# A hybrid decoder step on one core: the second chunk's rows loaded ahead of the value weights, the extra tokens' gates from float32 weights, maxima and first gates in another PSUM group

## The chip, the core and the metric

The kernel runs on one core of one Trainium2 chip. The core has five engines that each take their instructions in order: TensorE (PE, matrix products), VectorE (DVE, elementwise work and reductions), ScalarE (ACT, activations and scaled copies), GpSimd (POOL) and SyncE (SP, which here issues all the transfers). Products land in PSUM, a small memory of eight banks; everything else lies in SBUF. Sixteen DMA engines move data between device memory and SBUF.

The metric is the device time of one execution in microseconds (us). "Before" is the median of three executions. A profile is one further execution, taken by the hardware profiler, and its span is the time from its first to its last instruction.

## What is computed

One layer of a decoder for 2048 prompt tokens in 16 chunks of 128, with 48 extra tokens: 32 sample tokens (8 sequences of 4) and 16 meta tokens. All have 1024 features. Each token is layer-normed and goes through one combined projection; half of the width is an mLSTM evaluated chunk by chunk, the other half is sliding-window attention; both are gated, projected out and merged with the residual. Cut to what matters here:

```python
hp = layer_norm(concat([meta, x_prompt]), ln0_g, ln0_b)
hs = layer_norm(x_sample, ln0_g, ln0_b)
mq, mk, mv, mo, mz, mi, mf, aq, ak, av, az = split_proj(h @ w_in + b_in)

def mlstm_chunk(state, q, k, v, log_i, log_f):      # log_i = mi, log_f = log_sigmoid(mf)
    c, n, m = state
    b = cumsum(log_f)
    dmat = where(causal, b[:, None] - b[None, :] + log_i[None, :], -inf)
    inter = b + m
    m_t = maximum(inter, max(dmat))                 # running-max stabiliser
    w, s_inter = exp(dmat - m_t), exp(inter - m_t)
    ...
```

The meta tokens form a leading chunk, so the state with which the first prompt chunk starts depends on their gates `mi`, `mf` (four heads each, eight columns of the projection). The sample tokens start from given states `st_c`, `st_n`, `st_m`.

## The kernel before

**Precision by splitting.** Most products are made in float16 with a high and a low part: a weight matrix is loaded in float32 into four staging tiles, its largest magnitude is found, and it is scaled by a power of two and split into two float16 halves. `prep_steps` (L242) does this: a reduction for each quarter on ACT (L257) or DVE (L259), `all_max` (L128) over the partitions, `pow2` (L118), then for each quarter a scaled copy on ACT (L271) and a subtraction on DVE (L274). `all_max` multiplies the identity by each partition's maximum (L134, into `dg`, one buffer), sends it through a float32 matmul with ones (L135) into a PSUM tile, and reduces that on DVE (L136).

**PSUM.** Eight banks are shared by four groups: `pj` (2 buffers, projections), `pt` (3, transposes, scores, maxima, gates), `px` (1, extra tokens) and `po` (2), which is first used at L639.

**Phase A** runs over the chunks: layer norm and transposition (`norm_x`, L392, two chunks ahead of their use), projections q, k, v, o and gates, and the mLSTM recurrence (`m_rows` to `m_kv`). Between its steps the work of the extra tokens and the preparation of the second phase's weights are interleaved (`jobs`, L1060). **Phase B** runs over the chunks again for the attention and the output projection.

**The start of phase A** is the part that the change touches. The first chunk's rows `x0` are normed (L443), transposed in float32 (L448, copies L449) and multiplied with the unsplit float32 weights (`proj32`, L413), since split weights don't exist yet. `a_proj(0, i, st)` (L417) does this for q, k, v and o with the staging tiles `stq`, `stk`, `stv`, `sto`. The first two lie in different pools: q's and v's staging share the four buffers of tag "stg", so v's loads (L551, L552) wait until q's tiles have been read. k's and o's have buffers of tag "w" (name `stage`).

The extra tokens `xe` are normed (L556), split (`split_e`, L382) and transposed by a DMA into `ET`; `proj_e` (L301) multiplies them with split weights, high and low part stacked in one product. Before, their gates are made in the same way: `proj_e(ge, ET, wg, 8, bg, t1, ps=pt)` (L578), after `wg` has been prepared (L569). Then come the log-sigmoid (`log_sigmoid_rows`, L465: 15 small DVE operations and an exponential), two transposes (L581, L582), the scans for meta and sample tokens (L588 to L614) with the load `mS` of the sample states (L599) and four stores of the new ones (L616), three transposes (L619) and `tok` (L621).

x0 itself is also split and transposed for later (L561 to L563, stored by L622) and its normed rows are stored (L564). `xs`, the buffer of incoming rows, has two buffers: x0 and xe take both, so x1 (L565, L566) waits for one of them.

**What sets the order.** The code is traced once and a planner then places every instruction: the earlier in the code the higher its rank, but work that is ready goes to an engine that is free. Loads written with `first` (L108) form a chain: each is issued on SP after the one before it. Transfers written with `dma` (L98) are free until `Order.anchor` is set (L567), and after that are issued behind the anchor.

Of the kernel before, what the change touches and what calls it, by code (L numbers as in the profile page):

```python
# [16 lines left out]
P = 128  # L17
D = 1024
# [23 lines left out]
def tile_hymba_step(  # L42
# [22 lines left out]
    def pt(shape):  # L65
        return psum("pt", shape, 3)
# [4 lines left out]
    def po(shape):  # L71
        return psum("po", shape, 2)
# [8 lines left out]
    def work(tag, shape, dt=F32, bufs=None):  # L81
        return mn.tile(shape, dt, tag=tag, name=tag, bufs=bufs or KB4.get(tag, 1))
# [10 lines left out]

    class Order:
        last = None
        anchor = None

    def dma(out, in_, start=None):  # L98
# [9 lines left out]
    def first(out, in_, start=None):  # L108
        start = start or S.dma_start
        if Order.last is None:  # L110
            Order.last = start(out=out, in_=in_).ins
            return
        with tc.issue_after(Order.last):
            c = start(out=out, in_=in_).ins
        Order.last = c
# [12 lines left out]
    def all_max(a, m):  # L128

        n = m.shape[1]  # L130
        ps = pt([P, n, P])
        for i in range(n):
            d = small("dg", P, bufs=1)
            V.tensor_scalar(d, ident, m[:, i:i + 1], None, op0=ALU.mult)  # L134
            T.matmul(ps[:, i], ones, d, start=True, stop=True)  # L135
        V.tensor_reduce(a, ps, axis=AX.X, op=ALU.max)  # L136
        return a
# [9 lines left out]
    def bias_tile(off, n, dma=dma):  # L147
        b = work("bias", [P, n], bufs=4)
        dma(b, b_in[0:1, off:off + n].partition_broadcast(P))
        return b  # L150
# [23 lines left out]
    def stage(n, tag="stg"):  # L174

        if tag == "w":
            t = wp.tile([P, KT, n], F32, tag="w", name="stage")
            return [t[:, 2 * i:2 * i + 2, :] for i in range(4)]
        return [work("stg", [P, 2, n]) for _ in range(4)]

    def load(st, src, parts=range(4), dma=first):
        for i in parts:
            dma(st[i], src[:, 2 * i:2 * i + 2, :])
# [7 lines left out]
    load(stq, w_a[0])  # L191
    xe = work("xs", [P, D])[:NE]
    first(xe, x_e)
    stk = stage(512, "w")
    load(stk, w_a[1])
    bA = [bias_tile(0, 512, first), bias_tile(512, 512, first)]
    tg = cst.tile([P, KT, 8], F32, name="tg")
    first(tg, w_g)
    bg = cst.tile([P, 8], F32, name="bg")
    first(bg, b_in[0:1, 2560:2568].partition_broadcast(P))  # L200


    caus = cs[:, C_CAUS:C_CAUS + P]
# [252 lines left out]
    def scale_qk(i):  # L456

        m = small("bd", 1)
        V.tensor_scalar(m, wA[i].mx, xnorm, 32.0, op0=ALU.mult, op1=ALU.mult)
        V.tensor_tensor(m, m, bqk[:, i:i + 1], op=ALU.add)  # L460
        a, b = pow2(m, f"pq{i}", 2.0 ** -40)
        s_qk.append(a)
        i_qk.append(b)
# [36 lines left out]
    def a_gate(n):  # L500
        c = ca[n]
        gts = small("gts", 8)
        if n == 0:
            ps = pt([P, 8])
            proj32(ps, lambda k: tg[:, k])
            V.tensor_tensor(gts, ps, bg, op=ALU.add)
            log_sigmoid_rows(gts, P, 0)
            return
        ps = pt([P, 16])
        for k in range(KT):  # L510
            T.matmul(ps, c.xT[:, k, :], wg.t[:, k].rearrange("p c n -> p (c n)"), start=(k == 0), stop=False,
                     skip_group_check=True)
        for k in range(KT):
            T.matmul(ps[:, 0:8], c.xT[:, KT + k, :], wg.t[:, k, 0], start=False, stop=(k == KT - 1),
                     skip_group_check=True)
        V.scalar_tensor_tensor(gts, ps[:, 8:16], wg.ev, bg, op0=ALU.mult, op1=ALU.add)
        V.scalar_tensor_tensor(gts, ps[:, 0:8], wg.ev, gts, op0=ALU.mult, op1=ALU.add)
        log_sigmoid_rows(gts, P, n % 2)
# [29 lines left out]
    bA[3] = bias_tile(1536, 512, first)  # L548
    wA[0] = prep("q", stq, 512, sums=(0, 1, 2))
    scale_qk(0)  # L550
    stv = stage(512)  # L551
    load(stv, w_a[2])  # L552
    bA[2] = bias_tile(1024, 512, first)
# [2 lines left out]
    ln0_(xe, NE, hl.rearrange("p c d -> p (c d)").bitcast(BF16)[:NE])  # L556
    split_e(EE[:, 0], xe, NE, s_x)
    dmat(ET, EE[:, 0])
    first(cs[:, P:], consts[:, P:])
    xT0 = work("xT", [P, 2 * KT, P], F16)  # L560
    A.activation(hl[:, 0], x0, AF.Copy, scale=s_x)  # L561
    V.scalar_tensor_tensor(hl[:, 1], x0, s_x, hl[:, 0], op0=ALU.mult, op1=ALU.subtract)
    dmat(xT0, hl.rearrange("p c d -> p (c d)"))  # L563
    dma(h_d[0], x0)  # L564
    x1 = work("xs", [P, D])  # L565
    first(x1, x_p[P:2 * P, :])  # L566
    Order.anchor = Order.last  # L567
    a_proj(0, 0, stq)
    wg = prep("g", [tg[:, 2 * i:2 * i + 2, :] for i in range(4)], 8)  # L569
    a_gate(0)  # L570
    last = proj_e(qe, ET, wA[0], 512, bA[0], t1)
    dma(e_d[:, 0], qe)
    wA[1] = prep("k", stk, 512, sums=(0,2))
    scale_qk(1)
    sc_qk = col()
    V.tensor_scalar(sc_qk, i_qk[1], QSC, None, op0=ALU.mult)
    a_proj(0, 1, stk)
    last = proj_e(ge, ET, wg, 8, bg, t1, ps=pt)  # L578
    log_sigmoid_rows(ge, NE, 1)
    pr = pt([P, 2, P])  # L580
    T.transpose(pr[:, 0, :NE], Gf[1][:NE, :], ident[:NE, :NE])  # L581
# [37 lines left out]
        T.transpose(ptr[:NE, i, :], rows[:, i, :], ident)  # L619
    tok = ea.take(12)[:NE].rearrange("p (c h) -> p c h", h=H)  # L620
    V.tensor_copy(tok, ptr[:NE, :, 0:P:32])  # L621
    dma(xT_d[0], xT0)  # L622
    dma(he_d, xe)
    a_proj(0, 2, stv)
# [450 lines left out]
        return int(done[0]) > a  # L1075

    extra = jobs()
    carry.mark = None

    def a_steps(n):  # L1080
# [427 lines left out]
```

## Time and profile before

| | us |
|---|---|
| median of three executions | 1077.33 |
| lowest, highest | 1075.49, 1078.78 |
| the profiled execution, its own time | 1080.81 |
| its span, first to last instruction | 1079.0 |
| mean granted TensorE clock, share of full speed | 0.984 |

The profile gives for each instruction its engine, the line of the kernel, the tile that it writes and those that it reads, its start, its duration, and what ended the idle time of its engine before it. `xs<-in_dram` is a transfer of device memory into the tile `xs`; "SPq" is the queue in which SP issues transfers. PE is TensorE's stream of matmuls and PEld its weight loads. A float32 matmul shows as two instructions. Matmuls are pipelined, so the time from one start to the next, not the duration, is what one costs in a row of them. The granted clock is the share of full speed at which TensorE was allowed to run.

### The profile page before, as it was taken

The page shows a single profiled execution, that of the slowest core. Times are in us where ns is not written, and L with a number is a line of the kernel's source. Part 1 is how long each engine was busy: PE and PEld are TensorE (multiplying, and loading weights), DVE is VectorE, ACT ScalarE, POOL GpSimd, SP SyncE. Part 2 cuts the span into 40 slices and gives each one's busy share as a digit, 9 for nine tenths or more (in the row PEclk, how much of TensorE's full clock was granted, in tenths as well). Part 3 has the DMA queues.
Part 4 walks back from the last instruction along what each step waited for, and adds up shares of the span by engine and source line. Part 5 has one row for each costly group of instructions (what it writes and reads, how often), then busy time and mean ns, then how long its engine had stood idle before and what let it go on. Part 6 is the DMA issues. An engine that isn't in the chain of part 4 may idle for free.

```text
span 1079.0 us, 17626 instructions
## 1 busy us (share of the span) xinstructions
PE 1035.4 (96%) x6391; PEld 573.5 (53%) x6391; DVE 730.5 (68%) x2057; ACT 442.6 (41%) x1112; POOL 254.0 (24%) x270
## 2 busy tenths in 40 slices
PE   6979998999999998998999999999999999999996
PEld 3435565655555554555564554555555555555553
DVE  5769666776867796877546686566666566666674
ACT  5646332244444445462234343433343433343430
POOL 2112231321120001113011141333322333322322
PEclk9998999999999998999999999999999999999998
DMA  9756447345785686655686455546445645545452
GB/s 323 202 141 164 110 120 173 97 126 145 232 235 143 190 239 168 208 132 145 232 265 112 79 131 127 137 119 126 102 123 125 132 115 131 110 110 131 113 122 63
DMA packets 245809, 161.83 MB, mean 150 GB/s; under 512 B 207945, under 2 KB 220953, under 8 KB 244409
## 3 DMA queue, kind: packets, MB, share of 16 engines
q1 hardware_dynamic: 245722, 160.70, 57.3%
q8 instruction: 50, 0.82, 0.3%
q14 instruction: 37, 0.30, 0.1%
HBM read 68.22 MB, written 43.58 MB: 104 GB/s over the span
## 4 chain that ended last, share of the span: by engine, by line
PE 65%; DMA 12%; DVE 11%; issue 5%; ACT 4%; POOL 1%; SPq 1%; DVEq 0%; ACTq 0%; POOLq 0%
PE pj L1341 15%; PE pj L299 13%; PE pj L296 12%; PE pj L297 12%; PE pt L1261 3%; DMA xT<-hl 2%; PE po L1314 2%; DMA ea<-in_dram 2%; DMA stg<-hl 1%; DMA kT<-kh 1%; DVE xs L380 1%; DMA wd_o<-w_o 1%; PE px L725 1%; ACT hl L323 1%; DMA da<-e_d 1%
## 5 line engine op out<-in xcount | busy, mean ns | idle before, releaser
L296 PEld LDWEIGHTS <-xT 128*128 128x128 f16 x992 | 98.0, 99 | 103.9 <-issue 7.5
L299 PEld LDWEIGHTS <-xT 128*128 128x128 f16 x992 | 97.0, 98 | 98.3 <-issue 2.9
L297 PEld LDWEIGHTS <-xT 128*128 128x128 f16 x992 | 98.0, 99 | 94.8 <-issue 4.3
L1341 PEld LDWEIGHTS <-EE 128*128 128x128 f16 x720 | 70.8, 98 | 80.3 <-issue 2.2
L1341 PE MATMUL pj<-w_o,EE 128*128 128x512 f16 x360 | 83.7, 384 | 0.0
L1341 PE MATMUL pj<-wr_o,EE 128*128 128x512 f16 x360 | 82.3, 379 | 0.0
L1268 ACT ACTIVATE SI<-SI,nb 128x272 f32<-128x272 f32 (+1 forms) x64 | 32.4, 507 | 66.1 <-DVE nb L1265 66.0
L325 POOL TENSOR_TENSOR lns<-lns,mhalf 128x1 f32<-128x1 f32 (+1 forms) x16 | 20.1, 1256 | 136.9 <-ACT lns L324 123.9
L296 PE MATMUL pj<-w_q,xT 128*128 128x512 f16 x120 | 46.4, 387 | 4.8 <-DMA xT<-hl 4.8
L1274 POOL TENSOR_TENSOR mhl<-SI,mhl 128x32 f16<-128x32 f32 x32 | 13.7, 430 | 157.3 <-ACT mhl L1273 157.3
L783 POOL TENSOR_TENSOR qs<-qT 128x512 f32<-128x512 f16 x16 | 23.2, 1453 | 113.5 <-DMA qT<-qh 50.1
L1268 ACT ACTIVATE g<-g,nb 128x272 f32<-128x272 f32 (+1 forms) x64 | 32.1, 503 | 42.7 <-DVE nb L1265 42.7
L296 PE MATMUL pj<-wr_z,xT 128*128 128x512 f16 x128 | 49.3, 385 | 0.0
L297 PE MATMUL pj<-wr_z,xT 128*128 128x512 f16 x128 | 49.2, 384 | 0.0
L296 PE MATMUL pj<-wr_az,xT 128*128 128x512 f16 x128 | 48.5, 379 | 0.0
L296 PE MATMUL pj<-wr_aq,xT 128*128 128x512 f16 x128 | 48.5, 379 | 0.0
L297 PE MATMUL pj<-wr_aq,xT 128*128 128x512 f16 x128 | 48.5, 379 | 0.0
L297 PE MATMUL pj<-wr_az,xT 128*128 128x512 f16 x128 | 48.5, 379 | 0.0
L296 PE MATMUL pj<-w_o,xT 128*128 128x512 f16 x120 | 47.3, 394 | 0.0
L297 PE MATMUL pj<-w_o,xT 128*128 128x512 f16 x120 | 47.1, 393 | 0.0
L1171 POOL TENSOR_TENSOR xs<-xs,gb 128x1024 f32<-128x1024 f32 (+1 forms) x16 | 42.8, 2675 | 15.4 <-DMA stg<-hl 9.3
L296 PE MATMUL pj<-w_v,xT 128*128 128x512 f16 x120 | 46.4, 386 | 0.0
(459 smaller groups left out, 2506.1 us busy)
## 6 DMA issues: line engine op xcount, KB each, us to landing
stg<-in_dram SPq DMA_DIRECT2D x28, 512.0 KB
xs<-in_dram SPq DMA_DIRECT2D x16, 512.0 KB
h_d<-xs SPq DMA_DIRECT2D x16, 512.0 KB
xT_d<-xT SPq DMA_DIRECT2D x16, 512.0 KB
xs<-h_d SPq DMA_DIRECT2D x16, 512.0 KB
xT<-xT_d SPq DMA_DIRECT2D x16, 512.0 KB
out_dram<-xs SPq DMA_DIRECT2D x15, 512.0 KB
hn_d<-g SPq DMA_DIRECT2D x16, 258.0 KB
```

Source lines behind the costliest of these rows:

```text
L296: T.matmul(ps, xT[:, k, :], w.t[:, k, 0, :n], start=(k == 0), stop=False)
L297: T.matmul(ps, xT[:, k, :], w.t[:, k, 1, :n], start=False, stop=False)
L299: T.matmul(ps, xT[:, KT + k, :], w.t[:, k, 0, :n], start=False, stop=(k == KT - 1))
L323: A.activation(junk[:, D:2 * D], x, AF.Square, bias=nmu, accum_out=ss)
L325: G.tensor_tensor(rs, ve, mhalf[:rows, 0:1], op=ALU.pow)
L783: G.tensor_tensor(c.qs, c.qT[:, 0], c.qT[:, 1], op=ALU.add)
L1171: G.tensor_tensor(z, z, lg[:rows], op=ALU.mult)
L1261: T.matmul(ps[:, lo:], c.qT[:, h], kTs[:, 2 * (h // 4) + x, lo:], start=(x == 0), stop=(x == 1))
L1268: A.activation(p[:, i, lo:], p[:, i, lo:], AF.Exp, bias=nb[:, h:h + 1], accum_out=sums[:, h:h + 1])
L1274: G.tensor_tensor(m[:, 1], p[:, :, 2 * P:], m[:, 0], op=ALU.subtract)
L1314: T.matmul(pso[:, h], l, r, start=False, stop=(i == len(last) - 1), skip_group_check=True)
L1341: T.matmul(ps, c.yT[:, a, :], w[:, k, t, :], start=(first and j == 0), stop=(last and j == len(mm) - 1))
```

## The change

- `all_max` takes its PSUM tile from `po` until a flag `Order.running` is set, which happens where phase A's loop begins, and from `pt` after that. The first chunk's gates (`a_gate(0)`) take theirs from `po`.
- The loads of the gate weights `tg`, their bias `bg` and the constants move ahead of the loads of k's weights and of the biases of q and k.
- x1 is allocated and loaded ahead of v's staging loads, and so ahead of the bias behind them; before, it came after these and after the constants. The anchor is set at the same place relative to x0's store; it is now v's bias, no longer x1.
- The extra tokens' gates no longer use `proj_e` with split weights. `xe` is transposed by eight TensorE transposes into one PSUM tile, copied by ACT to `xef`, and multiplied with the float32 weights `tg` in eight matmuls; DVE adds the bias.
- This part, with the log-sigmoid, the scans, `mS`, the stores and `tok`, now stands ahead of x0's split and transposition, of the first chunk's q and k projections and of the preparation of the gate and k weights; before, it stood behind them.

```diff
--- before.py
+++ after.py
@@ -93,6 +93,7 @@
 
     class Order:
         last = None
+        running = False
         anchor = None
 
     def dma(out, in_, start=None):
@@ -128,7 +129,7 @@
     def all_max(a, m):
 
         n = m.shape[1]
-        ps = pt([P, n, P])
+        ps = (pt if Order.running else po)([P, n, P])
         for i in range(n):
             d = small("dg", P, bufs=1)
             V.tensor_scalar(d, ident, m[:, i:i + 1], None, op0=ALU.mult)
@@ -191,13 +192,14 @@
     load(stq, w_a[0])
     xe = work("xs", [P, D])[:NE]
     first(xe, x_e)
-    stk = stage(512, "w")
-    load(stk, w_a[1])
-    bA = [bias_tile(0, 512, first), bias_tile(512, 512, first)]
     tg = cst.tile([P, KT, 8], F32, name="tg")
     first(tg, w_g)
     bg = cst.tile([P, 8], F32, name="bg")
     first(bg, b_in[0:1, 2560:2568].partition_broadcast(P))
+    first(cs[:, P:], consts[:, P:])
+    stk = stage(512, "w")
+    load(stk, w_a[1])
+    bA = [bias_tile(0, 512, first), bias_tile(512, 512, first)]
 
 
     caus = cs[:, C_CAUS:C_CAUS + P]
@@ -501,7 +503,7 @@
         c = ca[n]
         gts = small("gts", 8)
         if n == 0:
-            ps = pt([P, 8])
+            ps = po([P, 8])
             proj32(ps, lambda k: tg[:, k])
             V.tensor_tensor(gts, ps, bg, op=ALU.add)
             log_sigmoid_rows(gts, P, 0)
@@ -548,6 +550,8 @@
     bA[3] = bias_tile(1536, 512, first)
     wA[0] = prep("q", stq, 512, sums=(0, 1, 2))
     scale_qk(0)
+    x1 = work("xs", [P, D])
+    first(x1, x_p[P:2 * P, :])
     stv = stage(512)
     load(stv, w_a[2])
     bA[2] = bias_tile(1024, 512, first)
@@ -556,26 +560,15 @@
     ln0_(xe, NE, hl.rearrange("p c d -> p (c d)").bitcast(BF16)[:NE])
     split_e(EE[:, 0], xe, NE, s_x)
     dmat(ET, EE[:, 0])
-    first(cs[:, P:], consts[:, P:])
-    xT0 = work("xT", [P, 2 * KT, P], F16)
-    A.activation(hl[:, 0], x0, AF.Copy, scale=s_x)
-    V.scalar_tensor_tensor(hl[:, 1], x0, s_x, hl[:, 0], op0=ALU.mult, op1=ALU.subtract)
-    dmat(xT0, hl.rearrange("p c d -> p (c d)"))
-    dma(h_d[0], x0)
-    x1 = work("xs", [P, D])
-    first(x1, x_p[P:2 * P, :])
-    Order.anchor = Order.last
-    a_proj(0, 0, stq)
-    wg = prep("g", [tg[:, 2 * i:2 * i + 2, :] for i in range(4)], 8)
-    a_gate(0)
-    last = proj_e(qe, ET, wA[0], 512, bA[0], t1)
-    dma(e_d[:, 0], qe)
-    wA[1] = prep("k", stk, 512, sums=(0,2))
-    scale_qk(1)
-    sc_qk = col()
-    V.tensor_scalar(sc_qk, i_qk[1], QSC, None, op0=ALU.mult)
-    a_proj(0, 1, stk)
-    last = proj_e(ge, ET, wg, 8, bg, t1, ps=pt)
+    xef = ea.take(8 * NE).rearrange("p (k t) -> p k t", t=NE)
+    ps = pt([P, 8, NE])
+    for j in range(8):
+        T.transpose(ps[:, j], xe[:, j * P:(j + 1) * P], ident[:NE, :NE])
+    A.activation(xef, ps, AF.Copy)
+    ps = pt([P, 8])
+    for k in range(KT):
+        T.matmul(ps[:NE], xef[:, k], tg[:, k], start=(k == 0), stop=(k == KT - 1))
+    V.tensor_tensor(ge, ps[:NE], bg[:NE], op=ALU.add)
     log_sigmoid_rows(ge, NE, 1)
     pr = pt([P, 2, P])
     T.transpose(pr[:, 0, :NE], Gf[1][:NE, :], ident[:NE, :NE])
@@ -619,6 +612,22 @@
         T.transpose(ptr[:NE, i, :], rows[:, i, :], ident)
     tok = ea.take(12)[:NE].rearrange("p (c h) -> p c h", h=H)
     V.tensor_copy(tok, ptr[:NE, :, 0:P:32])
+    xT0 = work("xT", [P, 2 * KT, P], F16)
+    A.activation(hl[:, 0], x0, AF.Copy, scale=s_x)
+    V.scalar_tensor_tensor(hl[:, 1], x0, s_x, hl[:, 0], op0=ALU.mult, op1=ALU.subtract)
+    dmat(xT0, hl.rearrange("p c d -> p (c d)"))
+    dma(h_d[0], x0)
+    Order.anchor = Order.last
+    a_proj(0, 0, stq)
+    wg = prep("g", [tg[:, 2 * i:2 * i + 2, :] for i in range(4)], 8)
+    a_gate(0)
+    last = proj_e(qe, ET, wA[0], 512, bA[0], t1)
+    dma(e_d[:, 0], qe)
+    wA[1] = prep("k", stk, 512, sums=(0,2))
+    scale_qk(1)
+    sc_qk = col()
+    V.tensor_scalar(sc_qk, i_qk[1], QSC, None, op0=ALU.mult)
+    a_proj(0, 1, stk)
     dma(xT_d[0], xT0)
     dma(he_d, xe)
     a_proj(0, 2, stv)
@@ -1075,6 +1084,7 @@
         return int(done[0]) > a
 
     extra = jobs()
+    Order.running = True
     carry.mark = None
 
     def a_steps(n):
```

## The prediction

> **What bounds the kernel now.** I read the page first, then the stretches (busy time of each engine), then TensorE's own waits, then the order of time in the first 100 us.
>
> ```profile
> span 1079.0 us, 17626 instructions
> PE 1035.4 (96%) x6391; PEld 573.5 (53%) x6391; DVE 730.5 (68%) x2057; ACT 442.6 (41%) x1112; POOL 254.0 (24%) x270
> ...
> 30.00:40.00 10.00, 10.00 (x45) 5.50 (x44) 6.47 (x13) 6.97 (x14) 0.95 (x1) 1.00 0.79 245
> 20.00:100.00 80.00, 70.31 (x303) 35.23 (x302) 64.71 (x172) 51.85 (x93) 12.64 (x8) 0.95 0.65 180
> ```
>
> TensorE (PE) is busy 1035 of 1079 us, so time can be won in two ways: less matmul work, or less idling. The change takes hardly any work away, so only the 44 us of idling count, and of these only those near the lines it touches. The columns of a stretch are its length, then PE, weight loads, DVE, ACT and POOL busy (with their instructions), the granted clock, the DMA share and GB/s. From 20 to 100 us PE is idle for 9.7 us and its mean clock is 0.95; DVE works 64.7 of the 80.
>
> ```profile
> PE pj L296 <- DMA xT<-hl: 4.8, 1, 4.8
> PE px L305 <- ACT w_v L271: 2.7, 1, 2.7
> PE po L642 <- DVE ws L769: 1.4, 1, 1.4
> PE pt L135 <- DVE cols L121: 0.5, 1, 0.5
> PE px L306 <- DVE w_v L274: 0.3, 1, 0.3
> ```
>
> These five waits of PE (total, times, longest) are all of that idling. The largest is for the second chunk's transposed rows, the next for the value weights. Three of them are followed by slow matmuls:
>
> ```profile
> 64.50:67.40 2.90, 2.90 (x7) 1.01 (x8) 0.00 (x0) 2.78 (x5) 0.00 (x0) 0.50 0.94 345
> 78.50:84.50 6.00, 3.06 (x7) 0.95 (x7) 4.52 (x11) 5.70 (x10) 0.00 (x0) 0.72 0.66 150
> 95.00:102.00 7.00, 5.78 (x22) 2.78 (x23) 7.00 (x22) 4.71 (x13) 1.29 (x1) 0.76 0.98 228
> ...
> 82.83 0.63 PE L305 MATMUL px<-w_v,EE 128*128 128x512 f16 x1
> 83.26 0.63 PE L306 MATMUL px<-w_v,EE 128*128 128x512 f16 x1
> ...
> 87.11 0.38 PE L305 MATMUL px<-w_v,EE 128*128 128x512 f16 x1
> 87.32 0.38 PE L306 MATMUL px<-w_v,EE 128*128 128x512 f16 x1
> ```
>
> A 128x512 matmul starts every 0.43 us after a gap (82.83, 83.26) and every 0.21 us otherwise (87.11, 87.32). Seven of them in the first stretch cost 7 x 0.21 = 1.5 us beyond the idling, seven in the second about as much, of which I count 1.4. In the third the missing clock is 7.0 x 0.24 = 1.7 us. So the three places hold 4.8 + 1.5 = 6.3 us, then 2.7 + 0.5 + 0.3 + 1.4 = 4.9 us, and 1.4 + 1.7 = 3.1 us: 14.3 us is all that can be won.
>
> [...]
>
> **The second chunk's rows.** How they come to be late is read from the order of time (start, duration, engine, line; in brackets the idle time before and what ended it):
>
> ```profile
> 30.38 3.91 SPq L114 DMA_DIRECT2D stg<-in_dram  x4
> ...
> 35.29 0.68 SPq L114 DMA_DIRECT2D xs<-in_dram  x1
> ...
> 44.05 1.06 ACT L321 ACTIVATE hl<-xs 128x1024 bf16<-128x1024 f32 x1 [1.32 <-DMA xs<-in_dram]
> ...
> 64.47 0.61 PE L296 MATMUL pj<-w_q,xT 128*128 128x512 f16 x1 [4.84 <-DMA xT<-hl]
> ```
>
> The load of x1 (xs at 35.29) stands on SP behind four loads of v's weights, which wait for q's staging buffers, and behind a bias and the constants. It lands 8.8 us after its issue, and its chain (two statistics passes on ACT, a power on POOL, three passes of DVE, a transposing DMA) takes another 20 us among other work on those engines. The change puts it ahead of those six. It can then go as soon as x0's buffer is free:
>
> ```profile
> 19.48 1.15 ACT L561 ACTIVATE hl<-xs,cols 128x1024 f16<-128x1024 f32 x1 [2.26 <-DVE xs L371]
> 19.56 0.33 SPq L101 DMA_DIRECT2D h_d<-xs  x1
> 21.94 1.27 DVE L562 SCALAR_TENSOR_TENSOR hl<-xs,cols,hl 128x1024 f16<-128x1024 f32 x1
> 28.00:32.00 4.00, 4.00 (x11) 1.85 (x10) 3.44 (x8) 4.00 (x4) 0.95 (x1) 1.00 0.47 88
> ```
>
> L562 ends at 23.2. The store h_d, issued at 19.6, lies behind the weight loads then under way; by 28 us these have drained (88 GB/s in that stretch). So I put x1's issue at 24 to 28, before a stretch in which the DMA engines are half idle, and its landing near 30: 14 us earlier. The gap asks for 5. The chain's three passes of DVE, 3 x 1.27 = 3.8 us, find 3.5 us of idling from 30 to 40 alone. I take the **first gap as closed: -6.3 us**; the least is 0. The six that x1 passes are held up only if x1 isn't ready before 30.38, which the second rival prices.
>
> **The extra tokens' gates.** Out go sixteen 128x8 f16 matmuls; in come eight transposes of 48 rows, a copy and sixteen f32 matmuls:
>
> ```profile
> 41.70 0.17 PE L305 MATMUL pt<-w_g,EE 128*128 128x8 f16 x1
> 41.73 0.17 PE L306 MATMUL pt<-w_g,EE 128*128 128x8 f16 x1
> ...
> 35.46 0.96 PE L415 MATMUL pt<-tg,wt 128*128 128x8 f32 x8
> 71.08 0.22 PE L582 MATMUL pt<-cs,Gi 48*128 48x48 f32 x1
> ```
>
> Out: 16 x 0.03 (start to start) = 0.4 us. The first chunk's own gate is the same product with 128 tokens for 48: 0.96 us for half of it, 1.9 in all. A 48x48 transpose shows 0.22 us with its pipeline's depth; in a row of eight I take half of that, 0.9 us. The sum is 0.9 + 1.9 - 0.4 = **+2.4 us**; between +0.9 (gate matmuls at the f16 pace) and +3.3 (no overlap of the transposes). PE is busy 10.00 of 10.00 in that stretch, so all of it lies on the path. ACT's copy and DVE's addition take the place of L308, L309 and L315 of the old helper: even.
>
> The gates' chain of 34 small DVE operations, at most 34 x 0.17 = 5.8 us by the row of L604 below, moves from around the first gap to before q's projection. DVE's 3.5 us of idling there take the larger part; some 2 us of other DVE work are pushed back, under PE's f32 matmuls, which need none of it. The chain also takes the state load `mS` and four small stores with it:
>
> ```profile
> 36.01 1.72 SPq L103 DMA_DIRECT2D ea<-in_dram  x1
> 44.27 0.17 DVE L604 COPY ea<-ea 128x8 f32<-128x8 f32 x1 [0.52 <-DMA ea<-in_dram]
> 75.97 3.33 SPq L103 DMA_DIRECT2D out_dram<-ea  x4
> 25.80 3.60 PE L415 MATMUL pj<-stage,wt 128*128 128x512 f32 x8
> ```
>
> `mS` landed 8.2 us after its issue, behind v's loads, and DVE, which takes its instructions in order, stood 0.5 us at L604 with everything behind it. Before, `mS` was held until x1 was issued; after, nothing holds it. I cost it at nothing. If it is queued behind v's loads while L604 has moved up, DVE stands up to 8.2 us, less the 3.5 of idling: +4.7, kept for the range. The four stores take 3.3 us of SP; at worst v's loads and the transposes behind them come that much later. Gates, bias and constants pass k's weights; PE first reads those at 25.80, after half of q's product, which hides the delay. Without that cover PE would wait for as long as the constants move, less than one of the 512 KB loads: about 1 us (3.91 / 4).
>
> **The two idle banks.** `all_max` wrote into `pt`, three buffers shared with the transposes:
>
> ```profile
> 20.65 0.60 ACT L449 ACTIVATE wt<-pt 128x512 f32<-128x512 f32 x1
> 21.26 0.63 PE L135 MATMUL pt<-dg,ones 128*128 128x128 f32 x2
> ...
> 44.82 0.28 DVE L134 TENSOR_SCALAR dg<-cs,mx 128x128 f32<-128x128 f32 x1
> ...
> 76.75 0.39 PE L135 MATMUL pt<-dg,ones 128*128 128x128 f32 x2
> ...
> 79.95 4.25 ACT L271 ACTIVATE w_v<-stg,cols 128x1024 f16<-128x1024 f32 x4
> ```
>
> q's maximum ran the moment L449 freed a buffer (20.65 + 0.60 = 21.25). v's operand was ready at 45.1 and its matmul ran at 76.75, 31 us later, with w_v's scaling behind it at 79.95. With `po`, idle until L639, neither waits for `pt`; w_v can be scaled before 60 us, and the second place loses its cause. What is late next is DVE: of the 80 us from 20 to 100 it works 64.7. Take 8 us out and it is at 64.7 / 72 = 90%; with 12 us, at 95%. So of the 4.9 + 3.1 = 8.0 us at the two later places I take half: **-4.0 us** (bounds -8.0 and 0).
>
> **The sum.** -6.3 + 2.4 - 4.0 = -7.9 us. The profiled execution took 1080.8 us, 1.8 of it outside the span, and would take 1072.9; it was 3.5 us above the median of 1077.3, so the forecast is 1077.3 - 7.9 = **1069.4 us**. Outside 20 to 100 us PE is busy (1035.4 - 70.3) / 999 = 97%, so it is the bound behind the change too, and a shift of the start should be carried to the end.
>
> **The rivals.** A measurement here tells about 0.3%, 3.2 us, from no change.
>
> All three places close: -6.3 + 2.4 - 8.0 = -11.9, **1065.4 us**. For it: the second chunk's products and the first chunk's recurrence, whose start state hangs on the gates, would all be at hand. Against it: DVE at 95%.
>
> Slower, by v's weights:
>
> ```profile
> 35.99 0.75 DVE L436 SCALAR_TENSOR_TENSOR qh<-q,cols,qh 128x512 f16<-128x512 f32 x1 [1.48 <-ACT qh L435]
> 40.63 1.22 DVE L259 TENSOR_REDUCE mx<-stg 128x1 f32<-128x1024 f32 x1 [1.14 <-DMA stg<-in_dram]
> 41.83 1.10 PE L415 MATMUL pj<-stg,wt 128*128 128x512 f32 x2
> ```
>
> On SP x1 now stands ahead of v's loads and waits for x0's buffer, and x0's last readers (L561, L562) are moved in the code behind the whole gate chain, next to q's projection. If they are placed there, near q's own split at 36, x1 issues at 37 and v's loads until 42. These landed 6.3 us after their last issue (34.3, 40.63), so now at 48; PE wants them at 41.8 + 2.4 = 44.2. That is 3.8 us idle, 1.5 of slow clock and 2.4 of new work, with the first gap no smaller: +7.7, or +3.7 if the later places give their 4.0. I price it at +5, **1082 us**. It decides once x1 issues after about 33. Against it: L561 ran as soon as its input was there, on an ACT that had idled 2.26 us, ahead of much lower line numbers; work is placed where an engine is free.
>
> Little changes: the rows come early, but their chain, last in the code, is squeezed by a DVE at over 90%, and half the first gap stays: -3.1 + 2.4 = -0.7, **1076.6 us**. About the same comes out if other things than the banks held the maxima (the change then doesn't do what it says) and the stall at L604 takes half of the first gap's 6.3.
>
> **How the numbers follow.** Forecast 0.45 (own range 1066 to 1074), all places 0.17, little 0.22, slower 0.16. Faster by over 0.3% (below 1074.1) is the first two: 0.62; within 0.22; slower 0.16. The range 1062 to 1081 leaves out the far part of the slower case (0.1) and of the fast one (0.05).
>
> **What would show it.** Right: x1's load issued before 30 and ahead of the four stg loads; its L321 near 32; no wait of L296 for xT; w_v's L271 before 70; PE idle under 6 us from 20 to 100 and still full until 60. Wrong: a wait of PE's v product for stg; DVE idle at L604 for over 2 us; a new wait of PE for the gates' operands before 60; or a gain at the start that is lost after 160 us, where the same work may be ordered anew.

## The result, and the profile after

| | before | after |
|---|---|---|
| median of 3 runs | 1077.33 us | 1063.49 us |
| range of the runs | 1075.49 to 1078.78 | 1059.23 to 1065.47 |
| ratio, 95% interval | | 0.9841 [0.9801, 0.9881] |
| profiled execution (its span) | 1080.8 (1079.0) | 1059.23 (1057.4) |

The change makes the kernel faster, by 1.6% by the ratio and by 13.8 us, 1.3%, by the two medians of three runs. A gain of 7.9 us, 0.7%, had been forecast: the direction was right and the time lies between 1062 and 1081, but the gain is about twice the forecast. The two profiled executions lie 21.6 us apart, more than the medians, because the one of before is slower than its three timed runs and the one of after is the fastest of its own. A second profile of the changed kernel (the first experiment, 1065.4 us) is therefore read beside it.

The page of after, its span and first line of engines:

```profile
span 1057.4 us, 17650 instructions
PE 1026.1 (97%) x6399; PEld 571.0 (54%) x6399; DVE 728.7 (69%) x2056; ACT 441.3 (42%) x1112; POOL 247.6 (23%) x270
```

The order of time of after (start, duration, engine, line, what is done, how often; in brackets the idle time before, with what ended it). Line numbers differ a little from the profile of before, L323 for the old L321, L597 for L604, L696 for L687:

```profile
27.97 0.37 SPq L115 DMA_DIRECT2D xs<-in_dram  x1
31.42 4.51 SPq L115 DMA_DIRECT2D stg<-in_dram  x4
33.67 1.04 ACT L323 ACTIVATE hl<-xs 128x1024 bf16<-128x1024 f32 x1
45.38 3.33 SPq L104 DMA_TRANSPOSE xT<-hl  x1
59.08 0.38 PE L298 MATMUL pj<-w_q,xT 128*128 128x512 f16 x1
59.94 4.25 ACT L273 ACTIVATE w_v<-stg,cols 128x1024 f16<-128x1024 f32 x4
...
82.87 0.17 DVE L696 COPY da<-ea 128x8 f32<-128x8 f32 x1 [1.66 <-DMA da<-in_dram]
85.54 0.17 DVE L696 COPY da<-ea 128x8 f32<-128x8 f32 x1 [1.53 <-DMA da<-in_dram]
87.72 1.50 DVE L261 TENSOR_REDUCE mx<-stg 128x1 f32<-128x512 f32 x2 [2.00 <-DMA stg<-in_dram]
90.99 0.73 DVE L430 SCALAR_TENSOR_TENSOR vaug<-pj,cols,bias 128x512 f32<-128x512 f32 x1
91.77 0.58 PE L298 MATMUL pj<-w_o,xT 128*128 128x512 f16 x1 [3.19 <-DVE vaug L430]
92.15 0.63 PE L299 MATMUL pj<-w_o,xT 128*128 128x512 f16 x1
92.58 0.63 PE L298 MATMUL pj<-w_o,xT 128*128 128x512 f16 x1
```

The load of x1 goes at 27.97, ahead of v's four; its transposed rows are on their way at 45.38, and PE's first product with them starts at 59.08 with no bracket: the 4.84 us gap is gone. The value weights are scaled from 59.94 on, where it was 79.95. A new gap stands at 91.77: PE waits 3.19 us for L430, and its next matmuls start 0.43 us apart. L430 was late on DVE, which takes its instructions in order and stood three times behind loads in the 10 us before (1.66, 1.53 and 2.00 us): the product that L430 reads was complete at 79.1, and L430 ran at 90.99.

The stretches of before, then of after (length, then PE, weight loads, DVE, ACT and POOL busy, the granted clock, DMA share, GB/s):

```profile
0.00:60.00 60.00, 50.59 (x158) 24.54 (x158) 42.44 (x116) 38.78 (x65) 11.42 (x25) 1.00 0.80 249
60.00:100.00 40.00, 30.69 (x162) 15.51 (x163) 31.13 (x86) 23.01 (x45) 6.80 (x5) 0.89 0.56 140
100.00:200.00 100.00, 95.39 (x594) 57.14 (x593) 70.83 (x220) 32.51 (x83) 26.21 (x18) 0.98 0.54 139
```

```profile
0.00:60.00 60.00, 52.22 (x173) 26.00 (x174) 45.18 (x137) 41.73 (x73) 11.54 (x26) 1.00 0.90 284
60.00:100.00 40.00, 35.61 (x193) 18.11 (x192) 33.25 (x79) 22.36 (x45) 4.12 (x5) 0.91 0.51 135
100.00:200.00 100.00, 99.73 (x646) 61.16 (x644) 71.65 (x230) 33.80 (x90) 27.56 (x20) 1.00 0.56 133
```

PE is busy 4.9 us longer in the 40 us from 60 on, and 4.3 us longer in the 100 us behind them, for which the prediction has no term but the last 2 us of its third place. All rows like these can be put into one sum. In each 20 us of the span I count what PE idles, and its busy time times the share of the clock that was not granted. The two together are its **lost time**. What is left of the span is then nearly the same: 1020.3 to 1022.7 us in before, after, e1_all and e3_gates_only, 1019.7 to 1024.4 over all kernels here. So the sum accounts for the differences to within a few us:

| lost time, us | 0 to 100 | 100 to 200 | 200 to 400 | 400 to 600 | 600 to end | sum |
|---|---|---|---|---|---|---|
| before | 22.1 | 6.7 | 1.4 | 14.2 | 13.7 | 58.2 |
| after, profile of 1059.2 us | 15.0 | 0.3 | 5.7 | 3.7 | 12.6 | 37.1 |
| after, profile of 1065.4 us | 14.5 | 0.8 | 5.8 | 7.1 | 13.4 | 41.6 |

The two profiles of the changed kernel agree within 0.5 us in each stretch until 400 us and differ by 3.4 us from 400 to 600. In the first 100 us the change loses 7.1 to 7.6 us less (10.3 had been forecast, -6.3 and -4.0), and in the next 100 us 5.9 to 6.4 less.

Behind 200 us the columns mislead, because they are cut at fixed times and the faster kernel does the same work earlier. Two rows of before:

```profile
199.36 0.93 PE L725 MATMUL px<-da 32*128 32x129 f32 x6
...
409.41 0.36 PE L511 MATMUL pt<-w_g,xT 128*128 128x16 f16 x8 [2.71 <-ACT am L764]
```

The same two in after, and in the second profile of the changed kernel:

```profile
184.62 0.93 PE L734 MATMUL px<-da 32*128 32x129 f32 x6
...
395.29 0.34 PE L513 MATMUL pt<-w_g,xT 128*128 128x16 f16 x8 [1.83 <-ACT am L773]
```

```profile
185.12 0.93 PE L734 MATMUL px<-da 32*128 32x129 f32 x6
...
395.81 0.35 PE L513 MATMUL pt<-w_g,xT 128*128 128x16 f16 x8 [2.71 <-ACT am L773]
```

The wait before 409.41 counts in the column from 400 before, and in the one from 200 after; nothing is given back between 200 and 400. Set side by side in the traces, PE's instructions from 182.8 us of before to its end (5594 of 6391) are the same lines on the same tiles (buffer numbers left out), in the same sequence, in the changed kernel. At 199.36 the changed kernel is 14.7 us ahead, 14.2 in its second profile, and at 409.41 it is 14.1 and 13.6 ahead. So the gain is complete by 200 us. What the spans show beyond that (21.6 and 15.4 us) differs between executions of one sequence.

### The profile page after: what moved, and what is told of

Its sections match the earlier page's. It is cut to its first block, busy times and chain, and to the rows that moved or that the text cites. A ratio compares the mean times of both kernels' runs of the same rounds, so it can differ in the third digit from the quotient of the medians.

```text
span 1057.4 us, 17650 instructions
## 1 busy us (share of the span) xinstructions
PE 1026.1 (97%) x6399; PEld 571.0 (54%) x6399; DVE 728.7 (69%) x2056; ACT 441.3 (42%) x1112; POOL 247.6 (23%) x270
## 4 chain that ended last, share of the span: by engine, by line
PE 69%; DMA 11%; DVE 10%; ACT 6%; issue 3%; POOL 1%; SPq 1%; DVEq 0%; ACTq 0%
PE pj L1351 14%; PE pj L301 14%; PE pj L298 14%; PE pj L299 14%; DMA stg<-hl 3%; PE pt L1271 3%; PE po L1324 2%; DMA stg<-in_dram 1%; DMA xT<-hl 1%; DMA kT<-kh 1%; ACT w_o L259 1%; DMA wd_o<-w_o 1%; DVE w_o L276 1%; PE po L816 1%; PE po L817 1%
## 5 line engine op out<-in xcount | busy, mean ns | idle before, releaser
L1284 POOL TENSOR_TENSOR mhl<-SI,mhl 128x32 f16<-128x32 f32 x32 | 12.6, 395 | 157.6 <-ACT mhl L1283 157.6
L793 POOL TENSOR_TENSOR qs<-qs,SI 128x512 f32<-128x512 f32 x16 | 20.9, 1307 | 113.5 <-ACT SI L784 113.3
L1181 POOL TENSOR_TENSOR xs<-xs,gb 128x1024 f32<-128x1024 f32 (+1 forms) x16 | 42.8, 2674 | 15.4 <-DMA stg<-hl 9.3
L298 PE MATMUL pj<-w_v,xT 128*128 128x512 f16 x120 | 46.0, 383 | 0.0
L299 PE MATMUL pj<-w_v,xT 128*128 128x512 f16 x120 | 45.8, 382 | 0.0
L792 POOL TENSOR_TENSOR qs<-qT 128x512 f32<-128x512 f16 x16 | 20.2, 1260 | 109.2 <-DMA qT<-qh 58.9
```

The costliest lines, as they stand in the source:

```text
L298: T.matmul(ps, xT[:, k, :], w.t[:, k, 0, :n], start=(k == 0), stop=False)
L299: T.matmul(ps, xT[:, k, :], w.t[:, k, 1, :n], start=False, stop=False)
L792: G.tensor_tensor(c.qs, c.qT[:, 0], c.qT[:, 1], op=ALU.add)
L793: G.tensor_tensor(c.qs, c.qs, c.SI, op=ALU.mult)
L1181: G.tensor_tensor(z, z, lg[:rows], op=ALU.mult)
L1284: G.tensor_tensor(m[:, 1], p[:, :, 2 * P:], m[:, 0], op=ALU.subtract)
```

## The experiments

My theory after the result, before the runs below: the early rows and the two banks close the places at the start, as forecast, and the rest of the gain comes from stages that only follow the start, through the order in which the planner puts the work. The rival: each part of the change has a price of its own, and these add up to the whole. The kernels before of the same sessions had medians of 1079.2 to 1080.3 us over 23 to 29 runs, and every ratio is to those.

### The parts alone

**The change as it is**, for a second profile and a tighter ratio.

> The changed kernel once more, with its own profile. The first profile showed 21.6 us less span than before, but the medians of the executions 13.8 us. Theory P (places): the start up to 200 us carries the gain (some 13 us of lost TensorE time, idle plus slow clock), the rest scatters from execution to execution; so the ratio comes out near 0.987, and in this profile the later stages (200 to 600 us) show another balance than +5.6 us. Theory O (order): the later stages were won by a new order of the work, so they show the same gain again, and the ratio is near 0.981.

1064.53 us, 0.9852 [0.9813, 0.9891]. The size holds; its lost time is in the table above. PE ran all its 6399 instructions in the same sequence as in the first profile, and behind 182.8 us that of before, so the later stages were not won by a new order: Theory O falls, and the start up to 200 us carries the gain, as in Theory P.

**Rows alone:**

```diff
     scale_qk(0)
+    x1 = work("xs", [P, D])
+    first(x1, x_p[P:2 * P, :])
     stv = stage(512)
...
-    x1 = work("xs", [P, D])
-    first(x1, x_p[P:2 * P, :])
```

> Before, with x1's load moved ahead of v's loads and nothing else. Theory P: the first gap (4.8 us idle, 1.5 slow clock) closes and the two later places stay: about -6 us, 1071. Theory T (tied): x1 lands early, but v's maximum still waits for pt and the gates for their old place, so the idling moves to the next wait: under 3 us. Theory O: any amount within 7 us, not explained by the first 100 us.

1076.28 us, 0.9972 [0.9946, 0.9997]. x1 was issued at 26.40 and the wait for xT is gone, yet only 3 us are won: v's maximum still ran at 74.14 and w_v was scaled at 76.68, and PE's waits until then are for other things. From 60 to 100 us it loses 13.6 us, as before (12.7).

**Block and float32 gates alone** (the whole diff but the early x1 and the two banks):

```diff
+    first(cs[:, P:], consts[:, P:])
     stk = stage(512, "w")
     load(stk, w_a[1])
...
+    xef = ea.take(8 * NE).rearrange("p (k t) -> p k t", t=NE)
+    ps = pt([P, 8, NE])
...
     xT0 = work("xT", [P, 2 * KT, P], F16)
...
     a_proj(0, 1, stk)
-    last = proj_e(ge, ET, wg, 8, bg, t1, ps=pt)
```

> Before, with the extra tokens' gates made from float32 weights and their block and loads moved forward, x1 and PSUM as before. Theory P: +2.4 us of TensorE work, and what the earlier start state gives back at the third place (at most 3.1): between -1 and +3 us. Theory T: the gap for x1 stays at 4 us or more. Theory O: any amount within 7 us.

1103.88 us, 1.0219 [1.0179, 1.0260]: 2.2% slower, the largest effect of the study, and more than Theory P or O allowed; of Theory T's wait for x1 nothing is left. The order of time of this kernel, and two of PE's waits (total, times, longest):

```profile
23.23 0.27 DVE L134 TENSOR_SCALAR dg<-cs,mx 128x128 f32<-128x128 f32 x1
...
64.25 0.29 PE L609 MATMUL pt<-cs,ea 128*48 128x128 f32 x1 [1.34 <-DVE ea L600]
64.38 0.39 PE L135 MATMUL pt<-dg,ones 128*128 128x128 f32 x2
...
65.62 0.28 DVE L134 TENSOR_SCALAR dg<-cs,mx 128x128 f32<-128x128 f32 x1
...
66.36 0.65 PE L135 MATMUL pt<-dg,ones 128*128 128x128 f32 x2
...
72.74 4.25 ACT L272 ACTIVATE w_k<-stage,cols 128x1024 f16<-128x1024 f32 x4
```

```profile
PE po L650 <- DVE vaug L316: 8.5, 1, 8.5
...
PE px L306 <- ACT w_k L272: 5.5, 1, 5.5
```

The first of these maxima is that of the gate weights, the second k's; the expectations of later runs take the first for k's. Its operand was ready at 23.5, and its matmul ran at 64.38. Between the two stands the block that moved: its tiles of `pt` come ahead of the maximum's in the code, and the three buffers are handed out in that order. L609, which writes the last of the block's tiles, starts at 64.25, and the maximum follows at once. k's operand needs `dg`, which has one buffer, and so is made only then (65.62). The key weights thus wait for the whole gate chain. The changed kernel, with the maxima in `po`, has the gate weights' on PE at 34.10 and k's at 41.45. The stretches of the slow kernel show what that costs:

```profile
60.00:100.00 40.00, 27.25 (x123) 13.06 (x121) 33.96 (x97) 26.55 (x42) 1.46 (x2) 0.79 0.44 115
100.00:200.00 100.00, 89.12 (x544) 54.20 (x545) 64.47 (x196) 30.65 (x86) 20.80 (x18) 0.91 0.45 114
```

PE is idle 12.8 us in the first of these and 10.9 in the second, and its clock is at 0.79 and 0.91.

**Banks alone:**

```diff
-        ps = pt([P, n, P])
+        ps = (pt if Order.running else po)([P, n, P])
...
-            ps = pt([P, 8])
+            ps = po([P, 8])
```

> Before, with all_max and the first gates in the po group and nothing else. Theory P: w_v is scaled before 70 us instead of at 80, the second place (4.9 us) closes, the first stays: -4 to -5 us, 1073. Theory T: no gain, since the first gap holds everything behind it: within 2 us. Theory O: any amount within 7 us.

1078.29 us, 0.9991 [0.9967, 1.0015]. w_v was scaled at 63.85, 16 us earlier, with nothing to show for it: w_q came at 34.71 instead of 27.85, x1 was issued at 43.22, and from 20 to 60 us, where before lost 0.4, it loses 4.3. Theory P was right about w_v and wrong about the time. A maximum that runs at once isn't a gain by itself.

### The parts in pairs

**Rows and gates**, without the banks:

> The change without the two PSUM banks: rows and gates moved, all_max and the first gates in pt as before. Theory S (slots are granted in the order of the code): with the gates' block ahead, its tiles in pt are in front of the maxima of k, v and o, as in the run with the gates alone (k's operand ready at 23, its matmul at 64), so the time stays near 1100 us. Theory T (the rows were missing): with x1 early the gates' block finds its cover and the time falls below 1080.

1098.75 us, 1.0173 [1.0147, 1.0200]. Theory S held. The operand of the gate weights' maximum was ready at 24.2 and its matmul ran at 62.03, k's at 65.08, and w_k was scaled at 72.16: the same mechanism as in the gates alone.

**Rows and banks**, with the block where it was:

> The change without the gates' block: rows first and banks. Theory S: banks only undo what the gates' block does to the maxima, so they add little to the rows: 1074 to 1077. Theory P (places): first gap and second place both close: -6.3 - 4.9 = -11, 1067.

1080.72 us, 1.0014 [0.9999, 1.0029]. Neither theory held. w_q came at 36.83, and 6.4 us are lost from 20 to 60.

**Gates and banks**, with x1 where it was:

> The change without the early rows. Theory S: gates and banks together give most of what the whole change gives, 1066 to 1070, since chunk 0's recurrence gets its start state early and fills the gap for x1. Theory P: the first gap is there again, so 5 to 6 us slower than the whole change: 1070 or more, with PE waiting 3 us or more for xT.

1078.38 us, 0.9985 [0.9965, 1.0004]. Theory S was wrong. x1 was issued at 36.03, and the first gap is back in the order of time:

```profile
64.04 0.61 PE L298 MATMUL pj<-w_q,xT 128*128 128x512 f16 x1 [4.72 <-DMA xT<-hl]
```

So with gates and banks in, the early load is what closes that gap. The ratios don't add: alone the parts give -0.3%, +2.2% and -0.1%, together -1.5%.

**All but the maxima's bank**, to tell the two uses of `po` apart (the first gates still go to `po`):

```diff
-        ps = (pt if Order.running else po)([P, n, P])
+        ps = pt([P, n, P])
```

> The whole change, but all_max back in pt; only the first chunk's gates use po. Theory S: it is the maxima that must not queue behind the block: near 1100 us, k's maximum after 60 us. Rival: it is the gates' tile that blocks pt: near 1065.

1084.96 us, 1.0041 [1.0022, 1.0059], between the two forecasts. The gate weights' maximum ran at 63.71, k's at 68.93, and w_k was scaled at 74.54. It is the maxima's bank that makes the early block bearable: with it 0.9852, without it 1.0041, and behind 182.7 us PE's sequence is that of before in both, so this is no matter of the later order. The first gates' tile in `po` makes a difference too (1.0173 without either).

**The block moved back**, float32 gates, rows and banks as changed (the sixteen lines from `xT0 =` to `a_proj(0, 1, stk)` again ahead of it):

> The whole change, but the extra tokens' gates (still from float32 weights) stand where the old ones stood, behind the k projection; loads, early rows and banks as changed. If the early start state is what the block gives: the first gap stays closed, the later waits come back, 1070 to 1076. If only the float32 weights matter (no wait for w_g) or the loads: as the whole change, 1064.

1079.46 us, 0.9991 [0.9976, 1.0006], slower than either forecast. It loses 15.4 us until 100, about as the change does, and then 6.5 to 200, where the change loses 0.3 to 0.8. The gain from 100 to 200 us is gone though only the order in the code is different. That raised the next question.

### The order by itself

The planner places the work of all later stages in one go. Does a move that neither adds nor removes work shift the time as much? The small load `mg` (four columns that scale part of the output weights) is put among the first loads, far ahead of its use.

```diff
     first(gbr, ln0.rearrange("(o c) d -> o (c d)", o=1))
+    mg = col(4)
+    first(mg, m_g)
...
-    mg = col(4)
-    dma(mg, m_g)
```

> The whole change, with one 2 KB load (mg, read much later) issued among the first loads; no work is changed, but the planner places most of the instructions of the loop otherwise. Theory P: the first 200 us lose 15 to 17 us of TensorE time as in both profiles of the changed kernel, and the time is 1061 to 1068. Theory O: the order decides, and the time goes anywhere between 1060 and 1080.

> The same null edit on the kernel before. Theory P: 1076 to 1082, with the first gap for xT still there. Theory O: off by up to 10 us either way.

With the changed kernel 1075.68 us, 0.9966 [0.9948, 0.9983]; with the kernel before 1079.61 us, 0.9985 [0.9968, 1.0003]. A move of one 4-column load took some 12 us of the changed kernel's gain away (0.9966 - 0.9852 of 1080). Theory P was wrong here: 25.3 us are lost in the first 200. PE's sequence is another one until 526 us, and only about 0.6 of the instructions from 100 to 200 us keep their place in it. The load's own delay is small: 8.4 us are lost before 20 us, 7.7 without the edit. In the kernel before the edit changes PE's sequence as much (about 0.5 keep their place), and the time stayed. PE's waits in the changed kernel so edited, and its stretches:

```profile
PE px L309 <- DVE vaug L319: 5.5, 1, 5.5
...
PE px L701 <- DMA da<-e_d: 2.9, 2, 2.0
...
PE po L834 <- DVE g L821: 2.7, 1, 2.7
```

```profile
0.00:60.00 60.00, 51.56 (x169) 25.70 (x169) 44.54 (x133) 38.93 (x68) 10.15 (x25) 1.00 0.89 275
60.00:100.00 40.00, 33.81 (x183) 17.35 (x181) 31.84 (x73) 23.74 (x44) 3.48 (x5) 0.91 0.57 148
100.00:200.00 100.00, 93.21 (x589) 56.34 (x590) 69.37 (x218) 32.53 (x83) 29.80 (x20) 0.98 0.50 130
```

The first gap stays closed and the stretch from 60 to 100 is still better than before (33.81 busy to 30.69), but from 100 to 200 PE idles 6.8 us, more than before's 4.6.

Three more moves of a store or a load, to see how far this goes. Put right behind `h_d`, the store `xT_d`:

```diff
-    dma(h_d[0], x0)
+    dma(h_d[0], x0); dma(xT_d[0], xT0)
...
-    dma(xT_d[0], xT0)
```

> The whole change, with the store of the first chunk's transposed rows (xT_d[0]) issued next to that of its normed rows instead of later: no work is changed, and the planner places most of the loop otherwise. If the 12 us between the changed kernel and its first neutral edit are the scatter of the order: anything from 1062 to 1078, and the lost TensorE time from 100 to 200 us decides it (0.5 us there gives 1064, 8 us gives 1076). If the first neutral edit hit one special spot: 1062 to 1067.

> The kernel before with the same neutral edit as e13: 1076 to 1082 (on this kernel the edit moves few instructions).

With the change 1070.45 us, 0.9936 [0.9912, 0.9960]; with before 1078.36 us, 0.9991 [0.9969, 1.0014]. The time of the first lies in the forecast scatter, but the stretch from 100 to 200 us did not decide it: 1.0 us is lost there. In before the edit changed nothing of PE's sequence behind 71.5 us, so the second is the kernel before once more. And `mg` behind bias 2, a move that leaves PE's sequence as it was:

> The whole change, with the 2 KB load of mg behind v's bias: a neutral edit that moves few instructions (a fiftieth of PE's order). Scatter of the order: close to the changed kernel, 1062 to 1068, as its order is nearly the same.

1064.71 us, 0.9871 [0.9842, 0.9900], the time of the unmoved kernel. Where the order stays, the time stays. Last, gates and banks without the early rows, with the edit of the first move, as the partner of e11_null_after:

> Gates and banks without the early rows, with the neutral edit of the mg load among the first loads. The pair with that edit on the whole change (ratio 0.9966) tells what the early rows are worth under another order: if they are worth their 6 us by themselves, this is 6 us slower than 1075.7, 1081 to 1083, with PE waiting 4 to 5 us for xT; if the 14 us between e7 and the whole change were the order, under 3 us slower.

1077.28 us, 0.9997 [0.9976, 1.0017]. The first gap is there, as it must be without the early rows:

```profile
PE pj L298 <- DMA xT<-hl: 5.6, 1, 5.6
```

The time is 1.6 us more than e11_null_after's, where 5.3 to 7.3 had been forecast if the rows were worth their 6 us alone. But the edit left PE's sequence that of e7_gates_banks from 82 us on, so the two kernels don't share an order, and their intervals overlap. The early rows are worth 0.3% between these two (0.9997 to 0.9966), 0.3% on top of the kernel before, and 1.3% between e7_gates_banks and the change (0.9985 to 0.9852). How much of each is the rows' and how much the order's, the runs don't separate.

### An attempt to go further

The new gap at 91.77 comes from DVE standing in order behind loads, at L696 (1.66 and 1.53 us) among other lines. Here the copy goes ahead of the load of its line:

```diff
-        dma(C3[:, :, 0:P], st_c[:, h].rearrange("b k v -> k b v"))
         V.tensor_copy(C3[:, :, P], ...)
+        dma(C3[:, :, 0:P], st_c[:, h].rearrange("b k v -> k b v"))
```

> The whole change, with the copy of the normaliser column (L696) ahead of the state load into the same tile (L695) in each of the four heads, so that DVE no longer stands behind that load (9.6 us in all from 60 to 200 us in the profile). Theory H (DVE held in order is the next bound at the start): the 3.2 us wait of PE for L430 and its slow clock shrink, -3 to -5 us, 1060. Rival: DVE goes on to stand at the next load (weights, 2.0 us), and nothing moves: within 2 us.

1071.99 us, 0.9915 [0.9898, 0.9933]. The stretch from 60 to 100 lost 6.6 us instead of 6.8 (after, profile of 1065.4 us); 3.3 us were lost from 100 to 200, and the whole was slower than the change: neither forecast held. This edit gives the planner another order too, so that it doesn't say what the stall itself is worth. No kernel of the study was faster than the changed one.

The kernels of this section, by their lost time:

| lost time, us | 0 to 100 | 100 to 200 | 200 to 400 | ratio |
|---|---|---|---|---|
| before | 22.1 | 6.7 | 1.4 | |
| e12_null_before | 22.8 | 5.4 | 4.4 | 0.9985 |
| e15_order2_before | 21.5 | 9.7 | 1.8 | 0.9991 |
| e1_all | 14.5 | 0.8 | 5.8 | 0.9852 |
| e14_small_order_after | 14.7 | 0.8 | 6.4 | 0.9871 |
| e13_order2_after | 18.5 | 1.0 | 6.1 | 0.9936 |
| e10_copy_first | 15.3 | 3.3 | 6.7 | 0.9915 |
| e11_null_after | 16.9 | 8.4 | 3.3 | 0.9966 |
| e9_block_late | 15.4 | 6.5 | 8.8 | 0.9991 |
| e7_gates_banks | 18.7 | 2.3 | 9.8 | 0.9985 |
| e16_order1_gates_banks | 17.6 | 5.4 | 7.8 | 0.9997 |

The first column splits: 21.5 to 22.8 for before and its two moves, 14.5 to 18.5 for the six kernels with the early rows, the float32 gates and the banks. Gates and banks without the early rows lie next to the latter, with 17.6 and 18.7. The other columns don't split. Before and e15_order2_before, with one sequence of PE, differ by 3.0 us from 100 to 200, so a single profile tells no less than that there.

## Where the prediction was right, and where it was wrong

**The second chunk's rows: right.** x1 was issued at 27.97, within the 24 to 28 that had been worked out, and its L323 (the old L321) stood at 33.67, where "near 32" had been put. The gap closed in every kernel with the early load and stayed, with 4.7 to 5.6 us, in the two of gates and banks without it. The condition of the slower rival, x1 issued after 33, never came.

**The gates: right in kind, too dear.** Two rows of after:

```profile
33.48 0.69 PE L566 MATMUL pt<-cs,xs 48*128 48x48 f32 x8
...
39.97 0.89 PE L570 MATMUL pt<-tg,ea 128*48 128x8 f32 x16
```

0.69 + 0.89 - 0.4 = 1.2 us of new work, not 2.4. Sixteen products with 48 tokens took 0.89 us, half of what the 128 tokens of L415 would (0.96 for eight); the product's price had been taken as if it didn't hang on the tokens. That no stall at L597 (the old L604) would come from `mS` was right: it was issued at 19.59 and was there when DVE got to it, at 28.64. PE stayed full from 20 to 60, as forecast.

**The banks: the earlier weights right, the reason and the worth wrong.** v's weights were scaled at 59.94, "before 60". But q's maximum, which was to run without waiting for L449's buffer, came at 27.15, later than before (21.26); w_q was scaled 1.0 us later (28.89 for 27.85). And the forecast took the banks' worth to be the second and third place's 4.0 us. The experiments show a larger role: without the maxima's bank the moved block holds k's weights up until 72.2 to 74.5 (e5_rows_gates, e8_gate_bank_only), and costs 2.2% alone. The prediction moved the block ahead of the maxima of the gate and key weights and didn't ask what the two share: both take their tiles from `pt`. With the maxima in `po` that does no harm.

**What is late next: right in kind, too small.** It named DVE, with half of the later 8 us left over. DVE's L430 is what PE waits for at 91.77, and from 60 to 100 PE idles 4.4 us; it had been said that 20 to 100 would idle under 6. But the new gap costs 3.2 us and 2.3 more by its eleven slow starts (11 x 0.21), and another wait 1.1, so 6.6 of the 8.0 us came back: the term of -4.0 measured -1.4.

**The step that failed: "14.3 us is all that can be won".** The prediction summed the three places up to 102 us and carried the shift unchanged to the end, since PE is the bound from there. Its terms measured -6.3, +1.2 and -1.4, or -6.5 us in place of -7.9. But the lead at 200 us is 14.2 to 14.7 us. The rest was won where the sum had no term: 1.2 to 1.3 us before 20 us (lost time 9.0 before, 7.8 and 7.7 after), and most of it from 100 to 200 us, where PE lost 6.7 before. Two of the waits of before in that stretch are

```profile
PE px L690 <- DMA da<-e_d: 2.5, 1, 2.5
...
PE px L725 <- DVE ea L706: 1.1, 1, 1.1
```

and after the change the first is down to 0.3:

```profile
PE px L699 <- DMA da<-e_d: 0.3, 1, 0.3
```

The lost time there falls by 5.9 to 6.4 us. That the forecast was short of the medians by about as much, 5.9 us, is chance, since two of its own terms were off too. The prediction named the opposite as a danger, "a gain at the start that is lost after 160 us, where the same work may be ordered anew", and gave it no term with both signs.

**How much of the 1.5% is the change's.** The first 100 us are: six kernels with its parts lose 14.5 to 18.5 us there, before and its two moves 21.5 to 22.8, 3 to 8 us more. Less the 1.2 us of added work that is 0.2 to 0.7% of the time, if the rest stays as it is. The gain from 100 to 200 us turns with the order: the change gives 0.9852 and 0.9871 in one order, 0.9936 and 0.9966 in two others, while the kernel before takes 0.9985 in a second order. With the change in, 0.8 to 8.4 us are lost in that stretch, for nothing but moved loads and stores. Yet the order in which it gains most is, behind 182.8 us, that of before. So 1.5% is what the change gives with before's order behind it, and 0.3 to 0.6% what it gave in two others. Which of its parts makes the gain from 100 to 200 us stays open: the runs that leave out a part changed the order too, but for the one without the maxima's bank (8.9 us lost there). Open too is whether the block's early place is worth anything itself: e9_block_late lost that gain, but so did e11_null_after, which had the block early.

## What to carry to other kernels

When an edit at the start shifts the work of a planner, the lost time of the stages behind it is up for grabs, in both directions: list all of it before setting a bound, not only what stands near the edit. Compare two profiles at the same instruction, not at the same time, or a wait that only comes earlier looks like a gain in one stretch and a loss in another. Before a gain of a per cent is put down to an edit, run edit and original each under a few moves that add and remove no work; what survives is the edit's. And when work is moved ahead in code, see which buffers it shares with what it now precedes: their order in the code can hold up an instruction whose input has long been there (here 41 us).

## What the hardware showed that was not expected

**Slow matmuls after short gaps.** In the order of time of after a gap of 3.19 us is followed by starts 0.43 us apart until about 96 us, and 0.21 to 0.22 us apart from 96.33 on. The prediction had found the same behind gaps of 2.7 and 1.4 us. The granted clock of after, around its gap from 88.58 to 91.77 (columns as above):

```profile
88.60:89.30 0.70, 0.00 (x0) 0.00 (x0) 0.70 (x2) 0.00 (x0) 0.00 (x0) 1.00 0.56 203
89.50:91.70 2.20, 0.00 (x0) 0.00 (x0) 2.20 (x5) 0.00 (x0) 0.00 (x0) 0.50 0.01 4
91.80:96.20 4.40, 4.40 (x11) 1.55 (x11) 3.52 (x17) 2.77 (x8) 1.27 (x1) 0.50 0.67 101
96.30:100.00 3.70, 3.70 (x19) 1.67 (x18) 3.55 (x7) 1.54 (x6) 1.89 (x1) 1.00 0.00 0
```

The clock fell 0.8 us into the gap. In before it fell 4.4 us into the first gap, of 4.84 us (64.0), at the end of the second (81.1), and 1.9 us after the third (98.1). In the traces of before and after the stretches at half clock, but for the one that the end of each cuts off, last 3.41 us (eight of them) or 6.83 us (two). The one from 98.1 on in before fell on a PE that was busy throughout, behind a gap of 1.43 us; by an estimate it cost 3.41 x 0.5 = 1.7 us. What sets such a stretch off isn't shown.

**Executions of one kernel spread.** The kernel before took from 1072.2 to 1086.4 us over the sessions, 1.3%, on top of what an order does. A difference of two profiles is worth no more than that, which is why the spans' differences behind 200 us were left open.
